# Experts' weights loaded 2 MB at a time into three slots, and other weights stored in whole pieces per partition

## Chip, cores and metric

The kernel runs on 1 core of one Trainium2 chip. The metric is the device time of one execution in microseconds. All inputs lie in the chip's memory (HBM) and are read once per execution, some 763 MB of them.

## What is computed

Two transformer blocks for one sequence of 256 tokens of 1024 features, in float32. The first block is attention and a mixture of 32 experts (each token goes to 4 of them). The second block has two layers, each with three branches (attention, a gated MLP over tokens, a convolution) and an MLP of width 4096; its first layer is also run for 256 context tokens, whose keys and values the latent tokens attend to. Cut to the parts that the change touches:

```python
def moe_ffn(h, ...):                       # 32 experts, top 4, blocks of tokens per expert
    logits = h @ w_router + b_router
    top_val, top_idx = lax.top_k(logits, 4)
    gates = softmax(top_val)
    for each block of tokens of one expert e:
        gu = xe @ w_gate_up[e] + b_gate_up[e]          # 1024 x 2048
        g = minimum(gu[:, :1024], 7); u = clip(gu[:, 1024:], -7, 7)
        act = (u + 1) * (g * sigmoid(1.702 * g))
        y = act @ w_down[e] + b_down[e]                # 1024 x 1024
    return sum over a token's experts of y * gate

def second_block(...):
    for l in range(2):
        p = h @ w_in[l]                                # 1024 x 8704
        x = x + g1 * rms_norm(mixer_merge(p, attn, ...))   # w_attn_o, w_gmlp_o, w_conv_o, w_out: 1024 x 1024
        x = x + g2 * rms_norm(square(relu(h2 @ w1)) @ w2)  # 1024 x 4096, 4096 x 1024
        # for l == 0 the same for the context tokens
```

## The kernel before

The kernel is written on a layer with named tiles in pools; a tag has a number of slots, a tile of a tag that has no free slot waits until the last reader of the oldest one is done, and the layer puts in the semaphores. It also puts each engine's instructions in an order at build time: by priority, and by a model of how long each instruction and transfer takes. On the chip each engine then runs its list in that fixed order. SyncE (SP) issues nearly all weight loads, also in a fixed order, so a load that waits for its slot holds up those behind it.

The work has three parts. The front (L473) is the first block's attention. The experts (`moe`, L998) follow, in the order of `SEQ`, in groups of at most 128 rows. 2 experts have room for 128 tokens, 16 for 64 and 14 for 32 (`CAPS`, sorted by the number of tokens they got; `overflow`, L1016, is run only if that does not suffice). Between the steps of the front and the experts, `prio` (L1702) lets the context pass (`ctx_pass`, L1368, self.side is True) emit its own steps, and gives the front and the experts the higher priority; the context's products are what TensorE does when an expert's weights are not there yet. When the context pass is through, self.solo is True and the experts may use its tiles too. The tail (self.tail) is two layers (`layer`, L1220) one behind the other.

The linear layers (`lin_steps`, L336) take their weights in blocks of 1024 x 512, 2 MB: `load_w` (L303) loads the block, `wsplit` (L317) splits its rows into a high and a low part (ScalarE writes `whi`, VectorE `wlo`; with an "s" at the end for the context pass), and TensorE makes three products of 256 columns of each 128 x 128 piece, at one pass each. A block is 96 such matmuls. The tiles of the weights are `raw` (three slots of 8 KB per partition, 1 MB), `raws` (three of 4 KB) and, for the context pass, `rawx` (one of 4 KB). In the front and in the experts' part a block is two `raw`, in the context pass four `raws` or `rawx`, in the tail one `raw` and two `raws`.

An expert's weights are not split; its products are plain float32. `expert_up` (L934) loads w_gate_up in 8 pieces of 128 rows, 1 MB each (`load_gu`, L917), and for each of them (k) issues the matmuls of L950; `expert_down` (L961) loads w_down in 4 pieces of 256 rows, 1 MB each (`load_dn`, L925), and issues those of L975 for each half of a piece. The tokens are the stationary side, so an expert of 32 tokens uses 32 of the 128 columns of the array, and its output columns go to four such groups side by side; one of 64 tokens uses two groups. The profile shows a float32 matmul as two instructions, so a 1 MB piece is 16 instructions for 32 tokens and 8 for 64 or 128.

`big` (L904) picks the slot of each piece in turn: two tiles of the pool mw (`raw3`, `raw4`) and the three of `raw`, five slots of 1 MB; if solo, five tiles of the context pass (`SPARE`) as well. The same `big` is:

```python
j = self.slot % (spare + len(MORE) + 3)
if j < spare:
    return self.t(self.cx, [P, 2048], tag=SPARE[j])
if j < spare + len(MORE):
    return self.t(self.mw, [P, 2048], tag=MORE[j - spare])
return self.t(self.raw, [P, 2048], tag="raw")
```

All weight matrices lie in HBM as the reference has them, row after row. The part of one partition in a transfer is then a row of 512 columns, 2 KB, for the linear layers, 8 KB (2048 columns) for w_gate_up and 4 KB (1024 columns) for w_down. Each such row is one packet of a DMA engine in the profile.

`combine` (L846) takes a group's results y, multiplies each row by its gate, splits it (`yh`, `yl`), and adds it up over tokens by matmuls against `G`, L873 and L874. `pad` (L117) is a tile that only moves the addresses of those behind it.

Of the kernel before, what the change touches and what calls it, by code (L numbers as in the profile page):

```python
# [98 lines left out]
class Builder:  # L99
    def __init__(self, tc, a, out, dbg=None):  # L100
# [4 lines left out]
        self.fbg = 0  # L105
        self.firstw = []
# [189 lines left out]
    def half(self):  # L296
        if self.side:
            self.hslot += 1
            if self.hslot % 4 == 0:
                return self.t(self.cx, [P, 1024], tag="rawx")  # L300
        return self.t(self.raw, [P, 1024], tag="raws")

    def load_w(self, w, q=None, parts=None):  # L303

        q = q or self.nc.sync
        parts = parts or (2, 1, 1) if self.tail else (1, 1, 1, 1) if self.side else (2, 2)
        rows, k0 = [], 0
        for h in parts:
            n = 2 * h
            r = self.t(self.raw, [P, 1024 * h], tag="raw") if h == 2 else self.half()  # L310
            r = r.rearrange("p (k n) -> p k n", k=n)
            q.dma_start(r, w[k0 * P:(k0 + n) * P, :].rearrange("(k p) n -> p k n", p=P))
            rows += [r[:, i:i + self.wn, :] for i in range(0, n, self.wn)]
            k0 += n
# [76 lines left out]
    def ada_pieces(self, w, b, sT, badd, mod, nv, slots=(), spool=None):  # L391
# [4 lines left out]
        def rows(k):  # L396
# [9 lines left out]
            for g0 in range(0, 4, ng):  # L406
                c0 = b * 2048 + g0 * 512
                r = self.half() if tag == "raws" else self.t(pool, [P, ng * 512], tag=tag, bufs=2 if tag == "gate" else None)
# [64 lines left out]
    def front(self, pool):  # L473
# [29 lines left out]
        w = a["w_in"][0]  # L503

        def project(sec, gi, dst):
            o = self.lin(w[:, sec * 512:(sec + 1) * 512], (hi, lo))
# [23 lines left out]
        def values(sec, v):  # L530
            o = self.lin(w[:, sec * 512:(sec + 1) * 512], (hi, lo), form="A")
# [129 lines left out]
        for s in range(2):  # L661
            o = self.lin(a["w_out"][0][:, s * 512:(s + 1) * 512], (ohi, olo))
# [241 lines left out]
    def big(self, solo):  # L904

        self.slot += 1
        if solo == "only":
            return self.t(self.cx, [P, 2048], tag=SPARE[self.slot % len(SPARE)])
# [107 lines left out]
    def overflow(self, pool):  # L1016
# [3 lines left out]
        with tc.If(anyv > 0):  # L1020
# [9 lines left out]
            with tc.For_i(0, NE, 1) as i:  # L1030
                cv = nc.values_load(self.ovi[0:1, bass.ds(i, 1)], min_val=0, max_val=T)
                with tc.If(cv > 0):
# [4 lines left out]
                    for t in range(2):  # L1037
                        brow = self.t(self.mw, [P, 2048], tag="raw3")
                        nc.sync.dma_start(brow[0:1, :], a["b_gate_up"][0][bass.ds(reg, 1), :])
                        h2 = self.t(self.mw, [P, 2048], tag="raw4")[:, :D].rearrange("p (k t) -> p k t", k=KC)  # L1040
# [179 lines left out]
    def layer(self, l, L, xT, pool, kall, vall, xs, pre=()):  # L1220
# [3 lines left out]
        w = a["w_in_2"][l]  # L1224
# [12 lines left out]
        for s in range(2):  # L1237
            ob = self.lin(w[:, 4608 + s * 512:5120 + s * 512], h, raws=early())
# [5 lines left out]
            oa = self.lin(w[:, 3584 + s * 512:4096 + s * 512], h, raws=early())  # L1244
# [5 lines left out]
        o = self.lin(w[:, 1024:1536], h, form="KV")  # L1250
# [7 lines left out]
        for s in range(2):  # L1258
            o = self.lin(w[:, 2560 + s * 512:3072 + s * 512], h, form="A")
            self.gv_evac(o, gv, gst, s)  # L1260
            o = self.lin(w[:, s * 512:(s + 1) * 512], h)
# [4 lines left out]
        for s in range(2):  # L1266
            o = self.lin(w[:, 1536 + s * 512:2048 + s * 512], h)
# [15 lines left out]
        def branch(goff, wo, acts, first, bg=0):  # L1283
            gts = [self.t(pool, [P, 4, T], tag="gate", bufs=2) for _ in range(2)]
            for s in range(2):
                o = self.lin(w[:, goff + s * 512:goff + (s + 1) * 512], h, bg=bg)
# [530 lines left out]
```

## Time and profile before

| | us |
|---|---|
| median of three runs | 2849.21 |
| lowest and highest | 2847.45, 2853.07 |
| the profiled execution's own time | 2844.92 |
| its span, from the first to the last instruction | 2842.8 |
| mean granted clock of TensorE, as a share of 2.4 GHz | 0.974 |

The profile is of one execution. PE is TensorE's matmuls, PEld its weight loads, DVE VectorE, ACT ScalarE, POOL GpSimd, SP SyncE. Busy time counts from an instruction's start to its end; the ends of matmuls are modelled, and neighbours overlap, so that the distance of two starts tells how fast they follow each other, not the duration. A wait is put down to the event that came last. A DMA share is the mean busy time of the 16 DMA engines over the stretch. L347 is the matmul of the linear layers, L950 and L975 are the experts', L324 and L325 the splits, L312, L921 and L929 the loads of `load_w`, `load_gu` and `load_dn`.

### The profile page before, as it was taken

The page shows a single profiled execution, that of the slowest core. Times are in us where ns is not written, and L with a number is a line of the kernel's source. Part 1 is how long each engine was busy: PE and PEld are TensorE (multiplying, and loading weights), DVE is VectorE, ACT ScalarE, POOL GpSimd, SP SyncE. Part 2 cuts the span into 40 slices and gives each one's busy share as a digit, 9 for nine tenths or more (in the row PEclk, how much of TensorE's full clock was granted, in tenths as well). Part 3 has the DMA queues.
Part 4 walks back from the last instruction along what each step waited for, and adds up shares of the span by engine and source line. Part 5 has one row for each costly group of instructions (what it writes and reads, how often), then busy time and mean ns, then how long its engine had stood idle before and what let it go on. Part 6 is the DMA issues. An engine that isn't in the chain of part 4 may idle for free. (4 is left out here: it accounts for less than half of the span.)

```text
span 2842.8 us, 50509 instructions
## 1 busy us (share of the span) xinstructions
PE 2695.5 (95%) x20396; PEld 2046.5 (72%) x20397; DVE 1635.6 (58%) x3105; ACT 1167.1 (41%) x1988; POOL 310.8 (11%) x300
## 2 busy tenths in 40 slices
PE   7999999999899999999999979899999998999898
PEld 5657777677566777664533338789888997899898
DVE  3564543868534424332321148999655789997655
ACT  2343343433233323221211126675544566666544
POOL 0000000000000000000000005545000045451000
PEclk9989999999799899999999989999999999999999
DMA  9767899899789998988899974435766544345352
GB/s 395 295 240 273 338 367 354 318 362 372 308 333 359 358 354 326 352 307 333 336 378 417 416 290 165 133 112 202 243 210 230 180 154 141 119 148 182 131 198 100
DMA packets 230015, 769.85 MB, mean 271 GB/s; under 512 B 14880, under 2 KB 15264, under 8 KB 189200
## 3 DMA queue, kind: packets, MB, share of 16 engines
q1 hardware_dynamic: 228384, 759.16, 71.9%
q0 software_dynamic: 1392, 7.41, 0.7%
q8 instruction: 162, 2.65, 0.4%
q14 instruction: 77, 0.63, 0.1%
HBM read 762.84 MB, written 3.67 MB: 270 GB/s over the span
## 5 line engine op out<-in xcount | busy, mean ns | idle before, releaser
L347 PE MATMUL lin<-hhi,wlo 128*128 128x256 f32 x1440 | 398.6, 282 | 22.8 <-DVE wlo L325 22.8
L347 PE MATMUL lin<-hhi,whi 128*128 128x256 f32 x1440 | 400.9, 282 | 3.3 <-ACT hhi L283 3.3
L347 PE MATMUL lin<-hlo,whi 128*128 128x256 f32 x1440 | 400.9, 280 | 0.1
L950 PE MATMUL mlin<-raw,hG 128*32 128x256 f32 (+2 forms) x2696 | 365.1, 474 | 3.5 <-DMA raw<-in_w_gate_up_dram 3.5
L325 DVE TENSOR_TENSOR wlo<-raw,whi 128x1024 fp32r<-128x1024 f32 (+1 forms) x232 | 268.0, 1157 | 133.7 <-ACT whi L324 124.5
L325 DVE TENSOR_TENSOR wlos<-raws,whis 128x512 fp32r<-128x512 f32 x246 | 167.9, 689 | 236.9 <-ACT whis L324 205.4
L324 ACT ACTIVATE whi<-raw 128x1024 fp32r<-128x1024 f32 (+1 forms) x232 | 217.8, 941 | 203.1 <-PE lin L347 126.5
L347 PEld LDWEIGHTS lin<-hhi,wlo 128*128 128x128 f32 x1440 | 269.8, 190 | 36.7 <-DVE wlo L325 32.5
L1532 POOL TENSOR_TENSOR yc<-yc,ctmp 128x256 f32<-128x256 f32 x240 | 256.1, 1091 | 296.4 <-ACT ctmp L1531 295.8
L324 ACT ACTIVATE whis<-raws 128x512 fp32r<-128x512 f32 x246 | 153.0, 630 | 313.4 <-PE side L347 297.5
L347 PEld LDWEIGHTS lin<-hhi,whi 128*128 128x128 f32 x1440 | 271.8, 190 | 7.9 <-ACT hhi L283 4.2
L347 PEld LDWEIGHTS lin<-hlo,whi 128*128 128x128 f32 x1440 | 272.9, 190 | 3.0 <-issue 1.4
L325 DVE TENSOR_TENSOR wlo<-raws,whi 128x1024 fp32r<-128x1024 f32 x164 | 206.5, 1259 | 106.5 <-ACT whi L324 106.1
L324 ACT ACTIVATE whi<-raws 128x1024 fp32r<-128x1024 f32 x164 | 174.1, 1062 | 186.4 <-PE lin L347 180.1
L950 PEld LDWEIGHTS mlin<-raw,hG 128*32 128x32 f32 (+2 forms) x2696 | 119.4, 123 | 141.0 <-issue 91.4
L347 PE MATMUL side<-hhi,whis 128*128 128x256 f32 x720 | 204.9, 289 | 0.5 <-ACT hhi L283 0.2
L347 PE MATMUL side<-hlo,whis 128*128 128x256 f32 x720 | 203.1, 286 | 0.0
L347 PE MATMUL side<-hhi,wlos 128*128 128x256 f32 x720 | 199.7, 290 | 1.1 <-DVE wlos L325 1.0
L975 PE MATMUL main<-raw,aT 128*32 128x256 f32 (+2 forms) x1368 | 185.8, 460 | 0.9 <-DMA raw<-in_w_down_dram 0.9
L1534 DVE SCALAR_TENSOR_TENSOR yc<-gl,cw,yc 128x256 f32<-128x256 f32 x240 | 170.9, 748 | 0.1
L347 PEld LDWEIGHTS side<-hhi,whis 128*128 128x128 f32 x720 | 136.9, 190 | 28.4 <-issue 22.6
L347 PEld LDWEIGHTS side<-hhi,wlos 128*128 128x128 f32 x720 | 132.8, 190 | 26.3 <-issue 18.8
(595 smaller groups left out, 5798.2 us busy)
## 6 DMA issues: line engine op xcount, KB each, us to landing
raw<-in_w_gate_up_dram SPq DMA_DIRECT2D x233, 1024.0 KB, 7.4
raw<-in_w_down_dram SPq DMA_DIRECT2D x115, 1024.0 KB, 8.2
raws<-in_w_in_dram SPq DMA_DIRECT2D x119, 512.0 KB, 3.7
raws<-in_w_ff_dram SPq DMA_DIRECT2D x112, 512.0 KB, 4.8
raw<-in_w_in_dram SPq DMA_DIRECT2D x48, 1024.0 KB, 5.2
raw<-in_w_ff_dram SPq DMA_DIRECT2D x32, 1024.0 KB, 5.5
phi<-in_ada_w_dram SPq DMA_DIRECT2D x10, 1024.0 KB, 7.5
plo<-in_ada_w_dram SPq DMA_DIRECT2D x10, 1024.0 KB, 7.1
```

Of the source, the lines that this page charges most:

```text
L324: x = nc.scalar.activation(flat(hi), flat(rows[i]), AF.Copy)
L325: y = nc.vector.tensor_sub(flat(lo), flat(rows[i]), flat(hi).bitcast(F32))
L347: x = nc.tensor.matmul(*args, skip_group_check=True, **kw)
L950: nc.tensor.matmul(d, hT(k), gu[k][c0 // D][:, c0 % D:c0 % D + W], start=False, stop=(k == KC - 1), skip_group_check=True)
L975: nc.tensor.matmul(pys[h][g * C:(g + 1) * C, :W], st, dn[m][:, c0:c0 + W], start=(m == 0), stop=(m == KC - 1), skip_group_check=True)
L1532: nc.gpsimd.tensor_add(d, d, m)
L1534: self.paced(1, nc.vector.scalar_tensor_tensor(d, x, wcol, d, op0=OP.mult, op1=OP.add))
```

## The change

It has four parts, here in the order of the code.

1. `load_gu` and `load_dn` load two k of w_gate_up, or four 128-row blocks of w_down, in one DMA of 2 MB. `big` gives three slots of 16 KB per partition: `raw3` in mw (in place of `raw3` and `raw4`) and two `raw`. The five tiles of the context pass, used when solo, stay at 8 KB and take one k or two blocks each.
2. Every weight matrix of the linear layers is stored in HBM as blocks of 1024 x 512 with each partition's 8 pieces one behind the other (`blocks`), and w_down with the four 128-row pieces of a half together. A partition's part of a transfer is then 4 KB for a `raws` piece, 8 KB for a 1 MB half of a block, 16 KB for w_down.
3. `load_w` takes a block as one 16 KB tile of `raw` in two DMAs of 1 MB; in the context pass as four small pieces as before; in the tail every third block as four small pieces and the others whole. `raw8` cuts a `raw` tile in two for the adaptive-norm weights.
4. The expert pool gets a pad of 64 bytes behind its first y tile, and the scratch of the software DMA queue is 4096 bytes instead of 8192.

```diff
@@ Builder
-    def load_w(self, w, q=None, parts=None):
+    def raw8(self):
+        if self.second is None:
+            x = self.t(self.raw, [P, 2, 2048], tag="raw")
+            self.second = x[:, 1, :]
+            return x[:, 0, :]
+        x, self.second = self.second, None
+        return x
+
+    def wblk(self, name, l, col, row=0):
+        return self.a[name][l, row // D, col // 512]
+
+    def load_w(self, w, q=None):
         q = q or self.nc.sync
-        parts = parts or (2, 1, 1) if self.tail else (1, 1, 1, 1) if self.side else (2, 2)
+        small = self.side
+        if self.tail:
+            self.nblock += 1
+            small = self.nblock % 3 == 0
+        whole = None if small else self.t(self.raw, [P, 4096], tag="raw")
         rows, k0 = [], 0
-        for h in parts:
+        for h in (1, 1, 1, 1) if small else (2, 2):
             n = 2 * h
-            r = self.t(self.raw, [P, 1024 * h], tag="raw") if h == 2 else self.half()
+            r = self.half() if small else whole[:, k0 * 512:(k0 + n) * 512]
             r = r.rearrange("p (k n) -> p k n", k=n)
-            q.dma_start(r, w[k0 * P:(k0 + n) * P, :].rearrange("(k p) n -> p k n", p=P))
+            q.dma_start(r, w[:, k0:k0 + n, :])
@@ setup
-        self.raw = st.enter_context(tc.tile_pool(name="raw", bufs=3))
+        self.raw = st.enter_context(tc.tile_pool(name="raw", bufs=2))
...
-            o = self.lin(w[:, sec * 512:(sec + 1) * 512], (hi, lo))
+            o = self.lin(self.wblk("w_in", 0, sec * 512), (hi, lo))
@@ big
-        j = self.slot % (spare + len(MORE) + 3)
+        j = self.slot % (spare + 3)
         if j < spare:
-            return self.t(self.cx, [P, 2048], tag=SPARE[j])
-        if j < spare + len(MORE):
-            return self.t(self.mw, [P, 2048], tag=MORE[j - spare])
-        return self.t(self.raw, [P, 2048], tag="raw")
+            return self.t(self.cx, [P, 1, 2048], tag=SPARE[j])
+        if j == spare:
+            return self.t(self.mw, [P, 2, 2048], tag="raw3")
+        return self.t(self.raw, [P, 2, 2048], tag="raw")
 
     def load_gu(self, eng, e, solo):
         gu = []
-        for k in range(KC):
+        while len(gu) < KC:
+            k = len(gu)
             r = self.big(solo)
-            eng.dma_start(r, self.a["w_gate_up"][0][bass.ds(e, 1), k * P:(k + 1) * P, :].rearrange("o p f -> p (o f)"))
-            gu.append([r[:, :D], r[:, D:]])
+            n = min(r.shape[1], KC - k)
+            eng.dma_start(r[:, 0:n, :], self.a["w_gate_up"][0][bass.ds(e, 1), k * P:(k + n) * P, :].rearrange(
+                "o (k p) f -> p (o k) f", p=P))
+            gu += [[r[:, i, :D], r[:, i, D:]] for i in range(n)]
         return gu
 
     def load_dn(self, eng, e, solo):
         dn = []
-        for j in range(4):
-            r = self.big(solo)
-            eng.dma_start(r.rearrange("p (k n) -> p k n", k=2), self.a["w_down"][0][
-                bass.ds(e, 1), j * T:(j + 1) * T, :].rearrange("o (k p) n -> p (o k) n", p=P))
-            dn += [r[:, :D], r[:, D:]]
+        while len(dn) < KC:
+            k = len(dn)
+            r = self.big(solo).rearrange("p a (k n) -> p (a k) n", n=D)
+            n = min(r.shape[1], 4 - k % 4)
+            eng.dma_start(r[:, 0:n, :], self.a["w_down"][bass.ds(e, 1), k // 4, :, k % 4:k % 4 + n, :].rearrange(
+                "o p k n -> p (o k) n"))
+            dn += [r[:, i, :] for i in range(n)]
         return dn
@@ moe
             y = self.t(pool, [P, D], tag="y")
+            if g == 0:
+                self.pad(pool, 64)
@@ host
+def blocks(z):
+    n, r, c = z.shape
+    return z.reshape(n, r // D, KC, P, c // 512, 512).transpose(0, 1, 4, 3, 2, 5)
...
+    for n in _BLOCKS:
+        host[n] = blocks(host[n])
+    host["w_down"] = host["w_down"].reshape(NE, 2, 4, P, D).transpose(0, 1, 3, 2, 4)
...
-    nc = bacc.Bacc("TRN2", target_bir_lowering=False, num_devices=1, dynamic_dma_scratch_size=8192)
+    nc = bacc.Bacc("TRN2", target_bir_lowering=False, num_devices=1, dynamic_dma_scratch_size=4096)
```

## Rows read from the trace of the kernel before

**Rows 1.** The page, part 1: busy us (share of the span) xinstructions

```profile
PE 2695.5 (95%) x20396; PEld 2046.5 (72%) x20397; DVE 1635.6 (58%) x3105; ACT 1167.1 (41%) x1988; POOL 310.8 (11%) x300
```

**Rows 2.** Stretches: length, busy time of each engine (instructions), PEclk, DMA share, GB/s

```profile
0.00:300.00 300.00, 271.38 (x1847) 190.16 (x1849) 154.79 (x537) 103.82 (x220) 6.75 (x22) 0.93 0.78 295
300.00:1450.00 1150.00, 1127.74 (x8819) 756.63 (x8820) 540.36 (x1166) 362.93 (x677) 1.31 (x4) 0.98 0.91 345
1450.00:1670.00 220.00, 200.63 (x962) 74.68 (x958) 40.74 (x78) 26.43 (x44) 0.00 (x0) 0.99 1.01 412
1690.00:2843.00 1153.00, 1086.94 (x8738) 1019.77 (x8738) 888.92 (x1308) 666.86 (x1037) 300.94 (x269) 0.98 0.49 165
```

**Rows 3.** Waits of TensorE, 300 to 1450: us in total, times, longest us

```profile
PE side L1576 <- DVE y L1534: 9.0, 1, 9.0
```

**Rows 4.** Waits of SyncE's queue, 300 to 1450

```profile
SPq L921 <- PE main L975: 178.1, 83, 7.1
SPq L921 <- PE mlin L950: 156.8, 72, 10.7
```

**Rows 5.** Timeline of TensorE: start, us, instruction, xcount, [idle before <-releaser]

```profile
1461.83 1.94 PE L950 MATMUL mlin<-raw,hG 128*64 128x512 f32 x8 [0.56 <-DMA raw<-in_w_gate_up_dram]
1464.32 1.94 PE L950 MATMUL mlin<-raw,hG 128*64 128x512 f32 x8 [0.54 <-DMA raw<-in_w_gate_up_dram]
```

**Rows 6.** Waits of TensorE and of SyncE's queue, 1690 to 2843

```profile
PE lin L347 <- DVE wlo L325: 28.6, 34, 1.8
...
SPq L312 <- DVE wlo L325: 770.9, 188, 22.5
```

**Rows 7.** Timeline of TensorE around one single run and one double run

```profile
319.16 0.28 PE L347 MATMUL side<-hhi,wlos 128*128 128x256 f32 x1
319.28 0.28 PE L347 MATMUL side<-hhi,whis 128*128 128x256 f32 x1
319.49 1.07 PE L950 MATMUL mlin<-raw,hG 128*32 128x256 f32 x16
320.49 0.39 PE L347 MATMUL side<-hlo,whis 128*128 128x256 f32 x1
320.71 0.28 PE L347 MATMUL side<-hhi,wlos 128*128 128x256 f32 x1
...
1004.73 0.28 PE L347 MATMUL side<-phi,wlos 128*128 128x256 f32 x1
1004.93 1.93 PE L950 MATMUL mlin<-raw,hG 128*32 128x256 f32 x32
1006.80 0.39 PE L347 MATMUL side<-phi,whis 128*128 128x256 f32 x1
1007.02 0.28 PE L347 MATMUL side<-plo,whis 128*128 128x256 f32 x1
```

**Rows 8.** Timeline of TensorE: first and last of the counted runs

```profile
465.99 1.94 PE L950 MATMUL mlin<-raw,hG 128*64 128x512 f32 x8
...
1183.65 1.07 PE L975 MATMUL main<-raw,aT 128*32 128x256 f32 x16
...
1442.49 1.94 PE L975 MATMUL main<-raw,aT 128*64 128x512 f32 x8
```

**Rows 9.** DMA issues, 300 to 1450: engine, op xcount, KB each, median us to landing

```profile
raw<-in_w_gate_up_dram SPq DMA_DIRECT2D x201, 1024.0 KB, 7.2
raw<-in_w_down_dram SPq DMA_DIRECT2D x96, 1024.0 KB, 7.6
```

**Rows 10.** Waits of ScalarE, 0 to 300

```profile
ACT whi L324 <- DMA raw<-in_w_in_dram: 6.5, 2, 5.5
```

**Rows 11.** DMA of the whole execution: a queue (packets, MB, share), issues (as rows 9)

```profile
q0 software_dynamic: 1392, 7.41, 0.7%
...
raws<-in_w_in_dram SPq DMA_DIRECT2D x119, 512.0 KB, 3.7
```

**Rows 12.** One line's instructions: durations in ns, min/median/max, first and last start

```profile
L873 PE MATMUL main<-G,yh x80: 277/282/388, 522.1 to 1456.9; 128*128 128x256 f32 x72, 64*128 64x256 f32 x8
```

More of the change, by code (lines that the diff above doesn't have):

```diff
@@ L105, in __init__ @@
         self.fbg = 0
+        self.nblock, self.second = 0, None
         self.firstw = []
@@ L407, in rows @@
                 c0 = b * 2048 + g0 * 512
-                r = self.half() if tag == "raws" else self.t(pool, [P, ng * 512], tag=tag, bufs=2 if tag == "gate" else None)
+                if tag == "raws":
+                    r = self.half()
+                elif tag == "raw":
+                    r = self.raw8()
+                else:
+                    r = self.t(pool, [P, ng * 512], tag=tag, bufs=2 if tag == "gate" else None)
                 x = nc.sync.dma_start(r, w[k * P:(k + 1) * P, c0:c0 + ng * 512])
@@ L530, in values @@
         def values(sec, v):
-            o = self.lin(w[:, sec * 512:(sec + 1) * 512], (hi, lo), form="A")
+            o = self.lin(self.wblk("w_in", 0, sec * 512), (hi, lo), form="A")
             for t in range(2):
@@ L661, in front @@
         for s in range(2):
-            o = self.lin(a["w_out"][0][:, s * 512:(s + 1) * 512], (ohi, olo))
+            o = self.lin(self.wblk("w_out", 0, s * 512), (ohi, olo))
             for j in range(2):
@@ L1223, in layer @@
         nc, a = self.nc, self.a
-        w = a["w_in_2"][l]
+        w = lambda c: self.wblk("w_in_2", l, c)
         v = 0
@@ L1243, in layer @@
                 self.kv()
-            oa = self.lin(w[:, 3584 + s * 512:4096 + s * 512], h, raws=early())
+            oa = self.lin(w(3584 + s * 512), h, raws=early())
             for j in range(2):
@@ L1306, in layer @@
         for s in range(2):
-            o = self.lin(a["w_out_2"][l][:, s * 512:(s + 1) * 512], (mhi, mlo))
+            o = self.lin(self.wblk("w_out_2", l, s * 512), (mhi, mlo))
             for j in range(2):
@@ L1362, in layer @@
             o = []
-            steps = self.lin_steps(o, a["w_in_2"][1][:, 1024:1536], self.hc, form="KV")
+            steps = self.lin_steps(o, self.wblk("w_in_2", 1, 1024), self.hc, form="KV")
             self.fill.extend([lambda: next(steps)] * 4)
@@ L1370, in ctx_pass @@
         nc, a = self.nc, self.a
-        w = a["w_in_2"][0]
+        w = lambda c: self.wblk("w_in_2", 0, c)
         v = 1
@@ L1397, in ctx_pass @@
         kc, vc = kvc[:, 0:2, :], kvc[:, 2:4, :]
-        o = self.lin(w[:, 1024:1536], h, form="KV")
+        o = self.lin(w(1024), h, form="KV")
         self.k_evac(o[0], L, kc, False, cx)
@@ L1413, in branch @@
                 yield
-                o = self.lin(wo[:, s * 512:(s + 1) * 512], acts)
+                o = self.lin(self.wblk(wo, 0, s * 512), acts)
                 self.merge(merged, gt, o, s, first)
@@ L1469, in ctx_pass @@
         for s in range(2):
-            o = self.lin(w[:, 2560 + s * 512:3072 + s * 512], h, form="A")
+            o = self.lin(w(2560 + s * 512), h, form="A")
             self.gv_evac(o, gv, gst, s)
@@ L1478, in ctx_pass @@
         yield from conv(1)
-        yield from branch(6656, a["w_gmlp_o_2"][0], (phi, plo), False)
+        yield from branch(6656, "w_gmlp_o_2", (phi, plo), False)
         phi, plo = pair()
@@ L1482, in ctx_pass @@
         yield
-        yield from branch(7680, a["w_conv_o_2"][0], (phi, plo), False)
+        yield from branch(7680, "w_conv_o_2", (phi, plo), False)
         phi, plo = pair()
@@ L1488, in ctx_pass @@
         for s in range(2):
-            o = self.lin(a["w_out_2"][0][:, s * 512:(s + 1) * 512], (phi, plo))
+            o = self.lin(self.wblk("w_out_2", 0, s * 512), (phi, plo))
             for j in range(2):
@@ L1507, in ctx_pass @@
                 c0 = f * D + s * 512
[L1508 removed]
+                o = self.lin(self.wblk("w_ff1_2", 0, c0), (hi, lo))
                 self.relu2(o, phi, plo, s, cx)
@@ L1750, in build @@
                         self.tail, self.wn = True, 2
-                        w = a["w_in_2"][0]
-                        pre = [self.load_w(w[:, 4608:5120]), self.load_w(w[:, 3584:4096], parts=(2, 2))]
+                        w = lambda c: self.wblk("w_in_2", 0, c)
+                        pre = [self.load_w(w(4608)), self.load_w(w(3584))]
                         self.tail = False
```

51 lines of the change are left out of this document (25 added, 26 removed).

## The prediction, put on record before the changed kernel was run

> **What bounds the kernel now.** I read the page's busy line first [rows 1]: matmuls cover 95% of the span, which by itself says little, since their ends are modelled. So I split the span into stages [rows 2]. From 0 to 300 us (front layer) the transfers run at a share of 0.78. From 300 to 1450 us the experts are worked through, with the context layer's products as filler ("side" tiles): matmuls are busy 1127.7 of 1150 us, transfers 0.91. From 1450 to 1670 us only experts are left: transfers are at 1.01 and 412 GB/s, matmuls have gaps. From 1690 us on the two tail layers run with transfers at 0.49.
>
> Then I asked, for each stage, which wait ends last. In 300 to 1450 TensorE's longest wait is one of 9.0 us behind VectorE [rows 3], and in that whole answer no row tells of a wait that a transfer ended. The other direction is full: SyncE's queue stands 178.1 + 156.8 = 335 us in front of w_gate_up loads until a matmul lets a slot go [rows 4]. So the weights are there early, and the stage lasts as long as TensorE's own stream of instructions. In 1450 to 1670 it is the reverse: every step of 1 MB begins after a wait for its load, and steps come 2.49 us apart though one lasts 1.94 us [rows 5]. In the tail it is TensorE, and VectorE's weight splits, 28.6 us in 34 waits; SyncE there waits 770.9 us for those splits [rows 6]. So only the middle stage and the experts-only stage can gain from the way in which experts are loaded.
>
> **Part 1: two steps of an expert per load (load_gu, load_dn, big).** What the middle stage's stream is made of shows in the timeline [rows 7]. Experts with 32 or 64 tokens use the array in 32- or 64-column tiles, the side products use all 128 columns. One load's worth of tiled work (16 instructions) stands between two runs of full-width ones. From the last side matmul before it (319.28) to the second after it (320.71) are 1.43 us: two side slots and 16 instructions. Where two loads' worth happen to stand together (x32), the same distance is 1004.73 to 1007.02 = 2.29 us. Side matmuls follow each other every 0.12 us (319.16, 319.28). Two single runs with their four side slots are 2.86 us; one double run, two side slots of its own and two more are 2.29 + 0.24 = 2.53 us. So each pair that is joined saves 0.33 us: that is what going into a tiled run and out of it costs.
>
> How many are there: in the timeline of 300 to 1450 us I count 125 runs of exactly x16 at 128*32 and 69 of exactly x8 at 128*64, both one load's worth; the first are at 319.49 [rows 7] and 465.99, the last at 1183.65 and 1442.49 [rows 8]. The unit is the load, not the step of the loop: for w_gate_up it is one k, for w_down two, and both give the same run length. The order on TensorE is written at build time by a planner that lets high-priority expert work in when its data should be there, so I expect the unit to follow the load: now two k, or four. 194 singles become 97 pairs: 97 x 0.33 = 32 us off a stage in which nothing else is late. Bounds: 0 (side matmuls still go in between the two halves) and, if longer runs form, half of all 273 tiled loads of the stage (297 loads [rows 9] less 24 of the two 128-token experts): 137 x 0.33 = 45 us. I take 32, because the rows show the load as the unit in both kinds.
>
> What comes due next: transfers would have to deliver the same bytes in 1118 us instead of 1150, a share of 0.94 for 0.91, less what longer rows save. That fits below the 1.01 of the experts-only stage.
>
> A 2 MB slot has to land whole before its first half is used, 1 MB more at 412 GB/s = 2.5 us later than now. Cover: three slots of 2 MB instead of five of 1 MB, so that between 4 and 6 MB stand ahead of TensorE instead of 4 to 5, and the queue's 335 us of standing still [rows 4]. I cost it at nothing; what it costs without cover is the slower rival.
>
> **Part 2: rows in whole pieces (blocks, wblk, the w_down layout).** Transfer time per byte follows from shares [rows 2]: the tail, nearly all 2 KB rows, moves 165/0.49 = 337 GB/s at full share; the experts-only stage, 8 KB and 4 KB rows, 412/1.01 = 408. After the change side weights come in 4 KB rows, tail and front weights in 8 KB, w_down in 16 KB. It pays only where transfers bind. In the 220 us from 1450 on, the 4 KB third becomes 16 KB: between 0 and 21% (the whole distance 337 to 408) of a third, 0 to 15 us; nearer to 0, as the step from 4 to 16 KB is the upper end of that distance. I take 5 us, less some 2 us, because one 1 MB step (1.94 us, [rows 5]) more remains behind the last landing: 3. In the front layer ScalarE waits 6.5 us for w_in in all [rows 10]: I take 2 us of 0 to 6.5, about the share that 8 KB rows save of a 2 KB row's time. In the middle and the tail nothing, since the queue waits for slots there.
>
> **Part 3: slots of the tail (load_w).** Two blocks of three come as one 16 KB tile, every third as four pieces in three slots, so its last piece can be issued only when its own first piece has been split, and the following blocks' loads stand behind it on SyncE. A block is four quarters of 24 matmuls at 0.12 us, so the piece is due 3 x 2.9 = 8.6 us after the first; such pieces land in 3.7 us [rows 11], with a 2 MB load at 412 GB/s in front in 8.8. I take 0, since the splits run up to three buffers ahead of TensorE; bounds -5 and, without that cover, some 27 such blocks (a third of the 83 of the two layers) x 1 us = +27 us.
>
> **Part 4: the small ones.** The 64-byte pad in the expert pool moves the combined results against their gates. The combine matmuls last 282 ns in the median and 277 at the least [rows 12]; with some 220 of them that is 1 us at most, either way: nothing. The smaller scratch of the software queue: its transfers are 0.7% of the engines' time [rows 11], 20 us spread over the span, and few are waited for: nothing, bound +5 us for one 1 MB transfer in line.
>
> **Sum.** 32 + 3 + 2 + 0 = 37 us. The profiled execution took 2844.9 us (span 2842.8 and 2.1 around it), 4.3 below the median of the three runs; against the median, 2849.2 - 37 = 2812 us.
>
> **Rivals.** (a) The forecast, 0.55: 2812, with its own bounds (20 to 45 for the joins, the rest as taken) 2799 to 2824.
> (b) Transfers, not TensorE, bind the middle stage, 0.12. For it: weight loads are busy only 756.6 of 1150 us there, against 1019.8 of 1153 in the tail [rows 2], so the array is not full. Against it: no wait on a transfer [rows 3]. Then joins give nothing, and the cheaper rows do: 345 GB/s x 1150 us less 297 loads of 1.05 MB leaves 85 MB of other weights, in 2 KB rows; going half the way from 337 to 408 GB/s they save 85 x (2.97 - 2.69) = 24 us; with 5 from the other stages 2820.
> The Trainium skill's page "Perfetto Trace Analysis", section "Identifying the Most-Contended Engine", speaks for this one: matmul busy time is not a good measure of TensorE, the busy share of its weight loads is, and by that 66% is not a bound. The waits are why I leave it at 0.12.
> (c) The runs do not join: the planner puts side matmuls between the halves as before, 0.18. Then 3 + 2 are left: 2844, half of it within 0.2%.
> (d) Slower, 0.15: the coarser slot starves TensorE. A slot is given back after two steps instead of one, SyncE stands in front of it twice as long, and the side weights queue up behind it. There are 297/2 = 149 such loads in the middle stage; from 0.25 us of TensorE idle per load (37/149) the gain is gone, at 0.5 us the time is 2812 + 74 = 2886. Against it: the 335 us of queue time, which is slack now.
>
> **How the numbers follow.** Faster or slower counts from 0.2% (5.7 us), about what a measurement of this kernel can tell from no change. Faster: 0.55 + 0.12 + 0.09 of (c) = 0.76. Same: 0.09. Slower: 0.15. The range takes in (a) to (c) with their bounds, from 2849 - 45 - 15 = 2789 up to no gain at all with 2 us of part 4, 2851; it leaves out (d).
>
> **What would show it.** Right: in the middle stage the tiled runs are x32 and x16 and about half as many; the start of the experts-only stage comes some 32 us earlier; distances within a run stay; the tail's length stays within 5 us. Wrong: single-step runs as many as now (c); a run count that halves while the stage keeps its length (b); rows of TensorE or of the side splits waiting for a transfer in that stage (d); or a tail that is longer by more than 10 us (part 3).

## The result and the profile after

The changed kernel takes 2814.15 us (median of 4 runs, 2808.83 to 2832.73), the one before 2849.53 us (median of 4). The ratio is 0.9894, with a 95% interval of 0.9869 to 0.9918: 30 us less, between 23 and 37 (the medians alone are 35 us apart). The prediction was 2812 us. The profiled execution took 2815.26 us, 29.7 us less than the profiled one of before.

In the changed kernel L365 is the matmul of the linear layers, L976 and L1001 are the experts', L342 and L343 the splits, L330, L944 and L955 the loads of `load_w`, `load_gu` and `load_dn`. First the stretches of the changed kernel, which answer to [rows 2] (columns as there):

```profile
0.00:300.00 300.00, 273.36 (x1821) 188.89 (x1823) 152.82 (x521) 104.79 (x221) 6.88 (x23) 0.93 0.75 290
300.00:1450.00 1150.00, 1117.00 (x8959) 765.14 (x8958) 549.52 (x1196) 366.96 (x682) 1.31 (x4) 0.98 0.91 357
1450.00:1670.00 220.00, 190.40 (x917) 78.24 (x916) 51.99 (x106) 33.94 (x57) 1.79 (x5) 0.94 0.91 375
1690.00:2843.00 1153.00, 1060.71 (x8538) 993.06 (x8536) 875.57 (x1274) 652.87 (x1020) 301.91 (x269) 0.99 0.44 161
```

Between 300 and 1450 us there are 140 more matmuls than before in the same time, at the same transfer share of 0.91 (357 GB/s for 345). Why shows in the timeline of TensorE (start, us, instruction, count), around the first loads of an expert; it answers to [rows 7]:

```profile
324.24 0.28 PE L365 MATMUL side<-hhi,wlos 128*128 128x256 f32 x1
324.35 0.28 PE L365 MATMUL side<-hhi,whis 128*128 128x256 f32 x1
324.56 1.93 PE L976 MATMUL mlin<-raw,hG 128*32 128x256 f32 x32
326.43 0.39 PE L365 MATMUL side<-hlo,whis 128*128 128x256 f32 x1
326.65 0.28 PE L365 MATMUL side<-hhi,wlos 128*128 128x256 f32 x1
```

Two steps stand together, and from the last side matmul before them to the second after them are 2.30 us, as for the rare double run of before (2.29). Counted from the timeline up to the last side product of a linear layer, there are 171 column-tiled runs of the experts' matmuls (with the bias products ahead of them); before there were 259. The single runs (x16 at 128*32, x8 at 128*64) are gone, but for one.

The waits in 300 to 1450 us, of TensorE on a transfer and of SyncE's queue on a slot (us in total, times, longest; the queue's answer to [rows 4]):

```profile
PE mlin L976 <- DMA raw<-in_w_gate_up_dram: 1.7, 3, 0.9
...
SPq L944 <- PE main L1001: 181.5, 42, 17.1
SPq L944 <- PE mlin L976: 144.1, 43, 9.1
```

By these two rows the queue still stands 326 us in front of w_gate_up loads (335 before), and TensorE waits 1.7 us for one.

When things begin and end, from the timeline of TensorE (starts, except where the row says end; us):

| | before | after | |
|---|---|---|---|
| first matmul of an expert | 309.5 | 324.6 | +15.0 |
| last side product of a linear layer | 1424.8 | 1415.4 | -9.4 |
| end of the last matmul of an expert | 1673.9 | 1644.4 | -29.5 |
| first matmul of the tail | 1693.5 | 1664.1 | -29.4 |
| end of the last matmul | 2834.0 | 2804.8 | -29.2 |

So the whole gain lies ahead of the tail: 24.4 us between the first expert's matmul and the last side product, 20.1 us in the experts-only stage behind it (249 to 229 us), and 15.0 us given back ahead of it.

### The profile page after: what moved, and what is told of

Its sections match the earlier page's. It is cut to its first block, busy times and chain, and to the rows that moved or that the text cites. A ratio compares the mean times of both kernels' runs of the same rounds, so it can differ in the third digit from the quotient of the medians.

```text
span 2813.5 us, 49773 instructions
## 1 busy us (share of the span) xinstructions
PE 2661.5 (95%) x20396; PEld 2045.3 (73%) x20397; DVE 1639.8 (58%) x3105; ACT 1167.3 (41%) x1988; POOL 311.9 (11%) x301
## 5 line engine op out<-in xcount | busy, mean ns | idle before, releaser
L343 DVE TENSOR_TENSOR wlo<-raw,whi 128x1024 fp32r<-128x1024 f32 (+1 forms) x288 | 337.4, 1174 | 160.4 <-ACT whi L342 153.2
L365 PE MATMUL lin<-hhi,wlo 128*128 128x256 f32 x1440 | 398.3, 283 | 20.8 <-DVE wlo L343 20.5
L365 PE MATMUL lin<-hhi,whi 128*128 128x256 f32 x1440 | 399.6, 281 | 2.2 <-ACT hhi L284 2.2
L365 PE MATMUL lin<-hlo,whi 128*128 128x256 f32 x1440 | 400.7, 280 | 0.1
L342 ACT ACTIVATE whi<-raw 128x1024 fp32r<-128x1024 f32 (+1 forms) x288 | 277.2, 964 | 257.9 <-PE lin L365 185.2
L976 PE MATMUL mlin<-raw,hG 128*32 128x256 f32 (+2 forms) x2720 | 348.3, 463 | 6.4 <-DMA raw<-in_w_gate_up_dram 6.3
L343 DVE TENSOR_TENSOR wlos<-raws,whis 128x512 fp32r<-128x512 f32 x246 | 167.7, 689 | 223.3 <-ACT whis L342 203.2
L365 PEld LDWEIGHTS lin<-hhi,wlo 128*128 128x128 f32 x1440 | 269.5, 190 | 36.2 <-DVE wlo L343 32.2
L365 PEld LDWEIGHTS lin<-hhi,whi 128*128 128x128 f32 x1440 | 271.5, 190 | 5.6 <-ACT hhi L284 3.7
L365 PEld LDWEIGHTS lin<-hlo,whi 128*128 128x128 f32 x1440 | 272.8, 189 | 2.8 <-issue 1.4
L342 ACT ACTIVATE whis<-raws 128x512 fp32r<-128x512 f32 x246 | 152.1, 629 | 280.1 <-PE side L365 246.2
L976 PEld LDWEIGHTS mlin<-raw,hG 128*32 128x32 f32 (+2 forms) x2720 | 126.8, 122 | 165.2 <-issue 117.4
L365 PE MATMUL side<-hhi,whis 128*128 128x256 f32 x720 | 203.4, 288 | 1.6 <-ACT hhi L284 1.1
L365 PE MATMUL side<-hlo,whis 128*128 128x256 f32 x720 | 200.3, 283 | 0.0
L365 PE MATMUL side<-hhi,wlos 128*128 128x256 f32 x720 | 193.7, 286 | 1.1 <-DVE wlos L343 1.0
L343 DVE TENSOR_TENSOR wlo<-raws,whi 128x1024 fp32r<-128x1024 f32 x108 | 138.4, 1281 | 71.6 <-ACT whi L342 70.8
L1001 PE MATMUL main<-raw,aT 128*32 128x256 f32 (+2 forms) x1336 | 174.0, 458 | 0.2 <-SPq L1048 0.2
L342 ACT ACTIVATE whi<-raws 128x1024 fp32r<-128x1024 f32 x108 | 114.5, 1060 | 122.4 <-PE lin L365 103.0
L365 PEld LDWEIGHTS side<-hhi,whis 128*128 128x128 f32 x720 | 136.3, 189 | 16.0 <-issue 11.3
L365 PE MATMUL side<-phi,whis 128*128 128x256 f32 x512 | 143.9, 287 | 2.2 <-ACT whis L342 1.8
```

Source lines behind the costliest of these rows:

```text
L342: x = nc.scalar.activation(flat(hi), flat(rows[i]), AF.Copy)
L343: y = nc.vector.tensor_sub(flat(lo), flat(rows[i]), flat(hi).bitcast(F32))
L365: x = nc.tensor.matmul(*args, skip_group_check=True, **kw)
L976: nc.tensor.matmul(d, hT(k), gu[k][c0 // D][:, c0 % D:c0 % D + W], start=False, stop=(k == KC - 1), skip_group_check=True)
L1001: nc.tensor.matmul(pys[h][g * C:(g + 1) * C, :W], st, dn[m][:, c0:c0 + W], start=(m == 0), stop=(m == KC - 1), skip_group_check=True)
```

## Experiments

The runs fall into three questions: is it the joined runs, what do they need, and what did the other parts do. In this table "runs" are the tiled runs up to the last side product, "gate_up by 1200" is the number of w_gate_up instructions on TensorE between 300 and 1200 us, "last side" and "last expert" are as in the table above, and the tail's length is from its first matmul to the end of the last one; all are counted from each kernel's timeline.

| kernel | ratio to before (95%) | runs | gate_up by 1200 | last side | last expert | tail's length |
|---|---|---|---|---|---|---|
| before | 1 | 259 | 2134 | 1424.8 | 1673.9 | 1140.5 |
| the change | 0.9894 (0.9869 to 0.9918) | 171 | 2176 | 1415.4 | 1644.4 | 1140.7 |
| e1: pairs, five slots of 1 MB | 0.9980 (0.9966 to 0.9994) | 143 | 2112 | 1258.4 | 1665.7 | 1145.0 |
| e2: single loads, three slots of 2 MB | 1.0013 (0.9996 to 1.0030) | 254 | 2176 | 1446.9 | 1677.5 | 1139.2 |
| e13: e2, y8 last | 0.9960 (0.9943 to 0.9977) | 254 | 2176 | 1448.2 | 1664.6 | 1141.4 |
| e5: single loads, six slots of 1 MB | 1.0049 (1.0020 to 1.0077) | 268 | 2176 | 1475.7 | 1684.5 | 1145.0 |
| e6: pairs, six slots of 1 MB | 0.9975 (0.9956 to 0.9995) | 178 | 2176 | 1420.9 | 1658.5 | 1142.7 |
| e12: e6, y8 last | 0.9896 (0.9874 to 0.9918) | 178 | 2176 | 1424.1 | 1645.4 | 1144.6 |
| e4: quads, three slots of 2 MB | 1.0450 (1.0420 to 1.0479) | 84 | 1984 | 1196.5 | 1803.3 | 1142.1 |

### e1: joined runs alone

`k` in the kernel before runs 1, 0, 3, 2, ...; `m` of w_down 2, 3, 0, 1, ...:

```diff
-        for k in range(KC):
+        for n in range(KC):
+            k = n ^ 1
...
-        for m in range(KC):
+        for n in range(KC):
+            m = n ^ 2
```

> The kernel before, with its 1 MB loads, its five slots and its old rows; only the order of the steps of an expert is changed: step 1 before step 0, 3 before 2, and so on (of w_down the second load's two steps before the first's). So the first matmul of a pair waits for the later of two loads, and the other step is ready behind it. In the order of TensorE's instructions there are then 144 column-tiled runs up to the last side product, against 260 before and 169 after. Theory J (what is saved is the way into and out of a tiled run, 0.33 us each): 116 x 0.33 = 38 us less than before, 2811 us, as fast as the change or faster, with none of its 2 MB loads and none of its layout. Rival L (the larger load or the slot is what helps): no change, 2849 us. Rival S (waiting for the second load of a pair starves TensorE): slower than before, by 0.25 us for each of about 150 pairs, 2886 us.

Measured: 2841.72 us, ratio 0.9980. The runs are joined (143 of them, fewer than in the change), and 6 us come of it, not 38: nearer to rival L (no change) than to theory J. Rival S (slower) falls. The stretches of e1, cut at its own last side product (columns as in [rows 2]):

```profile
309.00:1258.00 949.00, 926.77 (x8005) 685.06 (x7998) 496.65 (x1051) 345.12 (x645) 0.77 (x3) 0.98 0.91 350
1258.00:1666.00 408.00, 360.93 (x1704) 142.18 (x1703) 78.91 (x168) 43.96 (x74) 0.54 (x1) 0.97 0.94 378
```

TensorE is through with the side products 166 us earlier than before, but the experts' steps come no earlier: by 1200 us 2112 instructions of w_gate_up are done, against 2134, and the 3000th matmul of the experts starts at 1170.5 us, against 1160.0. The rows of that line alone, in 300 to 1200 us, of before, e1 and the change (length, PE, PEld, PEclk, DMA share, GB/s):

```profile
300.00:1200.00 900.00, 229.57 (x2134) 83.98 (x2135) 0.97 0.92 350
...
300.00:1200.00 900.00, 205.55 (x2112) 85.12 (x2112) 0.98 0.92 354
...
300.00:1200.00 900.00, 229.95 (x2176) 96.08 (x2176) 0.98 0.92 361
```

So the saved time was filled with side products ahead of their turn. When these had run out, 1184 of the experts' 4416 matmul instructions were left, against 784 before and 704 in the change, and the experts were then alone for 407 us instead of 249, with matmuls busy for 361 of 408 us. The saving was real and was given back in the next stage. Theory J as it stood (fewer switches, shorter kernel) falls: it needs a condition.

### e2 and e13: the change without joined runs

Each 16 KB slot is filled by two loads of 1 MB, so that a step can start with its own half (`load_dn` likewise):

```diff
-            eng.dma_start(r[:, 0:n, :], ...[bass.ds(e, 1), k * P:(k + n) * P, :]...)
+            for i in range(n):
+                eng.dma_start(r[:, i:i + 1, :], ...[bass.ds(e, 1), (k + i) * P:(k + i + 1) * P, :]...)
```

> The changed kernel with its three 16 KB slots and its layout, but each slot is filled by two loads of 1 MB, so that a step can start when its own half is there. The order of TensorE then has 253 tiled runs up to the last side product, against 169 of the changed kernel. Theory J: 84 x 0.33 = 28 us more than the changed kernel, 2842 us. Rival L (fewer slots of double size, or the layout, bring the gain and the runs do not matter): 2814 us, or faster, since the first half is there earlier.

Measured: 2851.25 us, 37 us over the change, with 254 runs: more than the 28 us of theory J; rival L (2814 us) falls. Here the experts are as early as in the change (2176 by 1200 us), but the last side product comes 31.5 us later. Part of the 37 us was something else: SyncE's queue stood 34.1 us in front of a load into y8, a tile that the context pass was still using, and TensorE then waited 11.1 us (waits from 1400 to 1500 us; `y` is y8, the view leaves numbers out):

```profile
SPq L945 <- DVE hks L1706: 34.1, 1, 34.1
...
PE mlin L978 <- DMA y<-in_w_gate_up_dram: 11.1, 1, 11.1
```

e13 takes that away by another order of the five context tiles (`SPARE`), with y8 first in the list, so that it is reached later:

```diff
-SPARE = ("phi", "plo", "hhi", "hlo", "y8")
+SPARE = ("y8", "phi", "plo", "hhi", "hlo")
```

> The changed kernel with two loads of 1 MB per 16 KB slot (2851 us), and the context pass's tiles in the order y8, phi, plo, hhi, hlo, so that the queue's 34.1 us in front of y8 and TensorE's 11.1 us behind it are gone. 253 tiled runs in the order. Theory J (the runs themselves cost 0.33 us each): 2851 - 11 = 2840 us, still 26 us over the changed kernel's 2814. Rival K2 (all that the single loads lost was that stop): 2814 us.

Measured: 2837.85 us, ratio 0.9960; expected 2840, and rival K2 (2814 us) falls. TensorE's long wait is gone; the queue still stands 11.7 us at that tile. Against the change that is 24 us for 83 more runs. The closer comparison is e14 below (2811.37 us), the change with the same order of the five tiles: it differs from e13 in the loads alone, and it is 26.5 us faster, 0.32 us per run. So with these slots the joins carry most of the change's gain; but joins were worth 6 us in e1. What differs is the slots.

### e5, e6 and e12: one MB more of slots

The kernel before with a fourth `raw` tile, six slots of 1 MB, first with single steps, then with the pairs of e1:

```diff
-        self.raw = st.enter_context(tc.tile_pool(name="raw", bufs=3))
+        self.raw = st.enter_context(tc.tile_pool(name="raw", bufs=4))
...
-        j = self.slot % (spare + len(MORE) + 3)
+        j = self.slot % (spare + len(MORE) + 4)
```

> The kernel before with a sixth slot of 1 MB for the experts (a fourth raw tile of 8 KB, paid for with the smaller scratch of the changed kernel); single loads of 1 MB, old rows, the tail's pattern as before (with four raw slots instead of three). 273 tiled runs in the order, against 260. Theory B (two bounds: the slots pace the experts, and TensorE's sum of work sets how late the side products end; one alone gives nothing): the 3000th matmul of the experts comes some 40 us earlier than before's 1160 us, as in the run with single loads (1118.6), but the last one ends within 6 us of before's 1674 us, as there (1677); the total is 2847 us, less what the fourth slot gives in the tail (0 to 11 us). Rival A (the slots alone are the gain): the experts end at about 1644 us, total 2817 us or less.

> The sixth slot and the paired order of steps together, still with loads of 1 MB, old rows and the old tail pattern; 183 tiled runs in the order. Theory B: both bounds move, and the experts end where they end in the changed kernel, at about 1644 us, 30 us earlier than before: 2817 us, or down to 2806 if the fourth slot helps the tail. Rival G (it takes loads of 2 MB, pairs of 1 MB loads don't do): as with pairs and five slots, 2842 us.

Measured: 2864.33 us for e5 and 2840.21 for e6, both above what theory B expected, and e6 where rival G has it. Yet the experts' pace did what it said: 2176 by 1200 us in both, as in every kernel with 6 MB of slots and steps in ones or twos, and the 3000th matmul of the experts at 1115 us. What came between shows in the waits of e6 from 1420 to 1500 us, of TensorE and of the queue:

```profile
PE mlin L951 <- DMA raw<-in_w_gate_up_dram: 17.2, 2, 16.0
...
SPq L921 <- DVE hks L1677: 29.2, 1, 29.2
```

The queue stands in front of the load into y8 until VectorE's last step of the context pass (hks); in e5 it stands 18.9 us there, and TensorE then waits 11.0 us. Behind it stand all other loads, though their slots are free: five `raw` loads go out right behind it (timeline of SyncE in e6: start, us, load, count):

```profile
1431.65 0.34 SPq L921 DMA_DIRECT2D hlo<-in_w_gate_up_dram  x1
1461.39 0.33 SPq L921 DMA_DIRECT2D y<-in_w_gate_up_dram  x1
1461.97 2.92 SPq L921 DMA_DIRECT2D raw<-in_w_gate_up_dram  x5
```

The transfers of e6 from 1435 to 1465 us, 40 slices of 0.75 us (busy tenths):

```profile
DMA  9999999999920000000000000000000000007399
```

They stand still for some 18 us (24 slices). In the kernel before and in e1 the queue comes to that tile when the context pass is long through; in e2, e5, e6 and e11, and for 5.2 us in the change, it does not. e12 is e6 with y8 moved:

```diff
-SPARE = ("phi", "plo", "hhi", "hlo", "y8")
+SPARE = ("y8", "phi", "hhi", "hlo", "plo")
```

> Six slots of 1 MB and pairs as in the run with both (2840 us), but the five tiles of the context pass come in another order (y8, phi, hhi, hlo, plo), so that the load into y8 is not the third of them: SyncE's queue stood 29.2 us in front of it there, until the context pass's last step was done, and TensorE then waited 16.0 us for w_gate_up. 183 tiled runs, as there. Theory K (joins and a sixth MB of slots are all that is needed; that stop is what took the gain back): no wait of more than 4 us on w_gate_up after 1420 us, the experts end at about 1643 us, 2840 - 16 = 2824 us. Rival G (loads of 2 MB are needed): 2840 us.

Measured: 2819.35 us, ratio 0.9896, 21 us less than e6 and the change's own 0.9894 again: loads of 1 MB, rows as before, the tail's pieces as before, no pad. TensorE's long wait is gone, though the queue still stands 12.0 us for hks, and the experts end at 1645.4 us, in the change at 1644.4. (The profiled execution of e6 was its fastest, 2831 us, so the traces show 13 of the 21 us.) Theory K holds and rival G falls: the change's gain takes neither 2 MB loads nor another layout, but joined steps, a sixth MB, and an order in which y8 does not stop the queue for long. Like for like it is not settled whether 2 MB loads and the layout add something: e14, with y8 first too, is 8 us faster than e12, and the two intervals overlap.

Side by side, against before: joins alone (e1) 6 us, 6 MB alone (e13, which has the new layout, too) 11 us, both (e12) 30 us. Together they give more than the sum of each alone.

### e4: longer runs

Pairs of 2 MB loads in the changed kernel:

```diff
-        for k in range(KC):
+        for n in range(KC):
+            k = n ^ 2
...
-        for m in range(KC):
+        for n in range(KC):
+            m = n ^ 4
```

> The changed kernel with the order of its steps swapped in pairs of loads: steps 2, 3, 0, 1, 6, 7, 4, 5 of w_gate_up, steps 4 to 7 before 0 to 3 of w_down. The first matmul waits for the second of two 2 MB loads, and four steps (eight of w_down) follow in one run. The order has 82 tiled runs up to the last side product against 169. Theory J: 87 x 0.33 = 29 us less than the changed kernel, 2785 us, faster than both. Rival S (coarser use of the three slots starves TensorE): two of the three slots are held until four steps are through, so only 2 MB stand ahead; with 75 such quads in the middle stage, 0.4 us of idle TensorE for each takes the gain back (2814), and 1 us makes it 2860.

Measured: 2977.36 us, 163 us over the change: rival S, and far beyond its 2860. There are 84 runs, half the change's, and only 1984 instructions of w_gate_up by 1200 us. The side products end at 1196.5 us, and the experts are then alone for 607 us. Of the experts' instructions 1536 are left at that point (704 in the change). TensorE's waits there, 1200 to 1800 us, and the stretch 1200 to 1700 us of e4 and then of the change (columns as in [rows 2]):

```profile
PE mlin L977 <- DMA raw<-in_w_gate_up_dram: 52.7, 16, 8.3
PE main L1003 <- DMA raw<-in_w_down_dram: 31.5, 8, 5.0
...
1200.00:1700.00 500.00, 388.18 (x1703) 160.59 (x1701) 74.48 (x166) 43.52 (x77) 0.54 (x1) 0.85 0.72 286
...
1200.00:1700.00 500.00, 467.15 (x2560) 244.13 (x2560) 155.65 (x291) 104.31 (x169) 9.93 (x14) 0.97 0.88 349
```

By the edit a quad holds two of the three slots until its four steps are through, and transfers are at 0.72 (0.88 in the change). The granted clock falls to 0.85 as well, so not all of the 163 us are waits. It is e1 once more, with less ahead.

### e3 and e15: the layout

e3 stores all weights as before in the changed kernel (the diff); e15 gives the kernel before the new layout (`blocks`, `wblk` and the w_down layout) and nothing else.

```diff
-            q.dma_start(r, w[:, k0:k0 + n, :])
+            q.dma_start(r, w[k0 * P:(k0 + n) * P, :].rearrange("(k p) n -> p k n", p=P))
```

> The changed kernel with all weights stored as before (rows of 2 KB for the linear layers' pieces, 4 KB for w_down); loads, slots and the order's 169 tiled runs stay. Theory J, with the prediction's part 2: 5 us in the experts-only stage and 2 in the front, 2814 + 7 = 2821 us; the middle stage and the tail keep their lengths within 3 us. Rival T (transfers bind the middle stage, too): 24 + 5 us, 2843 us. A tail that is longer by x us would say that the layout paid for x us of part 3 there.

> The kernel before with the changed layout of the weights alone: five slots, single loads of 1 MB, the tail's pieces and the scratch as before, no pad. 260 tiled runs in the order, as before. By the prediction's part 2: 5 us in the experts-only stage and 2 in the front, 2847 - 7 = 2840 us. Rival R (the change with old rows was 13 us slower, and that is the rows' price): 2834 us. Rival N (those 13 us were the slower pace of TensorE, 117.8 instead of 113.3 ns per matmul, at the end of that run; rows are worth nothing): 2847 us.

Measured: e3 2826.87 us (0.9921, interval 0.9896 to 0.9946), e15 2846.80 us (0.9991, interval 0.9976 to 1.0005). e15 says 2.6 us, between 7 and none, so rival R (13 us) falls; rival T of e3 (2843 us) falls, too. The 13 us of e3 lie, in its profiled execution, in the tail alone: its experts end at 1644.4 us as in the change, its tail is 1151.8 us long, and up to the 5760th matmul of the tail it is as fast (886.5 against 886.2 us). From there on each matmul is slower, as the section on the hardware shows. The intervals of e3 and of the change overlap, so the layout's worth is not settled closer than by e15.

The tail's stretch 1690 to 2800 us of before and of e15 (columns as in [rows 2]) shows that the rows' length did nothing there:

```profile
1690.00:2800.00 1110.00, 1055.51 (x8467) 988.96 (x8468) 867.78 (x1276) 652.04 (x1017) 298.90 (x267) 0.99 0.50 169
...
1690.00:2800.00 1110.00, 1058.58 (x8474) 991.58 (x8475) 867.73 (x1268) 652.08 (x1017) 300.06 (x267) 0.98 0.51 169
```

With 2 KB rows the transfers are at 0.50 and 169 GB/s, with 4 and 8 KB rows at 0.51 and 169. Share and rate in this stretch do not come from the rows' length.

### e8, e11 and e14: the tail's pieces, and the rest

e8 gives the changed kernel's tail its old pieces of 1, 0.5 and 0.5 MB:

```diff
-        if self.tail:
-            self.nblock += 1
-            small = self.nblock % 3 == 0
...
-        for h in (1, 1, 1, 1) if small else (2, 2):
+        for h in parts or ((2, 1, 1) if self.tail else (1, 1, 1, 1) if self.side else (2, 2)):
```

> The changed kernel, but the tail's blocks come in the pieces of the kernel before (1 MB, 0.5, 0.5), the 1 MB piece as half of a 16 KB tile. The experts and the layout are those of the change. Theory P3 (the change's slots in the tail cost some 11 us, which its layout gives back: with the old rows its tail is 11 us longer than before's): the tail, from the first tail matmul to the last, falls from 1140.7 to about 1129 us, total 2803 us. Rival (the tail is bound by TensorE and the splits, whatever the slots): 2814 us.

Measured: 2810.75 us (0.9874, interval 0.9845 to 0.9903); its tail is 1141.3 us long, the change's 1140.7. Theory P3 was built on e3's long tail, and falls with it: the tail does not depend on the pieces.

e11 is e6 with the new layout (and the change's tail rows in the old pieces).

> Six slots of 1 MB with single loads, paired order of steps, the changed layout, the tail's pieces of before: the change without its 2 MB loads and without its tail pattern. 183 tiled runs in the order. Theories B and P3 together: experts' end at about 1644 us, tail of about 1129 us, 2803 us, faster than both kernels by 11 us or more. Rival G (2 MB loads are needed): 2830 us (the pairs with five slots, 2842, less 11).

Measured: 2840.93 us (0.9973). That is above both theories. It is e6 again, with the same stop (29.3 us of the queue, 16.1 us of TensorE), and the layout did not make up for it. What it was meant to tell, e12 tells.

e14 is the change with the `SPARE` of e13.

> The changed kernel with the context pass's tiles in the order y8, phi, plo, hhi, hlo; all else as it is, 169 tiled runs in the order. In the changed kernel the queue stands 6.2 us in front of the load into y8, and the transfers idle there. Theory W (in the experts-only stage transfers bind, so what the queue waits is lost): 2814 - 6 = 2808 us. Rival (the next wait, 13.0 us for a gather's matmuls, ends last anyway): 2814 us.

Measured: 2811.37 us (0.9863, interval 0.9841 to 0.9884), the lowest ratio of all kernels here. Against the change's 0.9894 it is 3 us of median or 9 of ratio, and the intervals overlap: the run does not decide between theory W and its rival. The change's stop at y8 was short (5.2 us of the queue), and in e14 it is gone. The smaller scratch and the pad were not tried alone: the larger slots need the scratch's room.

## Why the prediction was right, and where it was not

**What bounds the kernel.** "The stage lasts as long as TensorE's own stream of instructions" [rows 3, 4] was half of it. That no transfer is waited for shows that TensorE hardly ever waits, not that less work on it ends the stage earlier: it can be filled with work that belongs later. e1 takes more runs away than the change does and gains 6 us. The Trainium skill's page "Perfetto Trace Analysis", section "Identifying the Most-Contended Engine", says that matmul busy time is no good measure of TensorE and the busy share of its weight loads is; by that the stage, with 756.6 us of them in 1150 [rows 2], had room. e1 agrees: its stage has 685 us of them in 949, 72% for 66%. Rival (b), for which the rule spoke, fell as it was priced (e15).

**Part 1, the price.** 0.33 us per join is right: 2.30 us for a double run in the change against two singles of 1.43 [rows 7], and 0.32 us of total time per run between e13 and e14, which differ in nothing else but the size of the loads. The Trainium skill's page "TensorEngine Tiling (Array Packing)", section "Key Properties", says that a change of tiling mode drains TensorE; it has no duration. These rows show what going in and out costs, but not whether a drain is the cause.

**Part 1, the count.** Predicted 97 joins, found 88 (259 to 171): 29 us for 32. The load as the planner's unit was right; e2 has 254 runs with the same slots and half the load.

**Part 1, the cover.** This is the step that failed, though the sum did not show it. "Three slots of 2 MB instead of five of 1 MB" was costed at nothing, as a risk without a price. It was the condition of the gain. By the prediction's own price e1 should have taken 2811 us, and it took 2842. With 5 MB of slots the written order lets 2112 to 2134 w_gate_up instructions in by 1200 us, with 6 MB 2176 (the 3000th matmul of the experts comes at 1160 us in the kernel before and at 1115 in the change), and only with these is there expert work to put into the time that joins set free. "What comes due next" asked whether transfers could follow (share 0.94; it is 0.91), and not whether the filler would run out.

**"The start of the experts-only stage comes some 32 us earlier".** Wrong: 9.4 us. By the prediction's own signs, a run count that falls while the stage nearly keeps its length pointed to (b). The experts start 15.0 us later (86 more matmuls of side products and a later routing ahead of them; which part of the change does that is open, e12 and e5 have 5.8 and 5.5 us of it), and the stage itself is 20.1 us shorter, because more of the experts' work is done by then (704 instructions left, 784 before). The prediction gave that stage 3 us.

**Part 2.** Predicted 5 us, measured 2.6 (none to 7). The size can stand, the reason cannot: the price of 2 KB rows was read from the tail's 337 GB/s at full share [rows 2], and e15 shows that share and rate stay with longer rows.

**Parts 3 and 4.** Predicted 0 for the tail, measured +0.2 us (1140.5 to 1140.7). The bound of +27 us was never near: old pieces or new, the tail keeps its length (e8, 1141.3). The combine matmuls' median is 280 ns against 282 [rows 12], nothing, as said.

**The rivals.** (c), no joins, would have been the result of e2. (b) fell as priced: e15 gained 2.6 us, not 24 and 5. That transfers do not hold TensorE's stream back in the middle stage shows in e1, which was through with the same side products 166 us earlier; the experts' own steps came no faster there. (d) did not come in the change (1.7 us of TensorE waiting for a load), but its mechanism is real: e4 shows its place and is 163 us slower. It decides when a run needs two of three slots.

So the total was right by some luck: the change brought the sixth MB along with the joins, and the prediction put nearly all of the gain down to the joins.

## What to carry to other kernels

Where one engine alternates two streams, time saved on it shortens the kernel only if the stream that ends last can use it: look at which stream runs out first, and give the loads of the other one more slot together with the saving. Joined runs need no larger transfers; swapping neighbouring steps of a sum, so that the later load is waited for first, does the same for a few lines. In a queue that issues loads in order, sort the slots by when they come free: one load into a tile still in use stopped all transfers for 18 us.

## What was not expected of the hardware

TensorE has two paces at the same granted clock. The timeline of the tail of the change, and then of e3; the two rows of each fence are 16 matmuls apart:

```profile
2729.74 0.28 PE L365 MATMUL lin<-shi,whi 128*128 128x256 f32 x1
...
2731.55 0.28 PE L365 MATMUL lin<-shi,wlo 128*128 128x256 f32 x1
```

```profile
2729.82 0.28 PE L365 MATMUL lin<-slo,whi 128*128 128x256 f32 x1
...
2731.70 0.28 PE L365 MATMUL lin<-shi,wlo 128*128 128x256 f32 x1
```

That is 1.81 us in the change and 1.88 in e3, 113 and 118 ns a matmul. The stretch 2700 to 2800 us of e3 and of the change (columns as in [rows 2]) has a granted clock of 1.00 in both, the 2.4 GHz level, and 851 against 880 matmuls:

```profile
2700.00:2800.00 100.00, 100.00 (x851) 100.00 (x850) 59.49 (x61) 46.63 (x52) 0.00 (x0) 1.00 0.44 153
...
2700.00:2800.00 100.00, 99.72 (x880) 99.52 (x879) 59.74 (x63) 47.74 (x57) 2.04 (x2) 1.00 0.39 145
```

In e3 the slower pace holds from about 2550 us to the end, and its tail is 11 us longer; in e5 it holds for the last 200 us. It does not come with the old rows in the tail: e14, which has the new ones, has it for the first 100 us of the tail, and the kernel before, with old rows, has both paces. This is the slower one there, at 2600 us (16 matmuls apart, 1.88 us):

```profile
2599.88 0.28 PE L347 MATMUL lin<-slo,whi 128*128 128x256 f32 x1
...
2601.76 0.28 PE L347 MATMUL lin<-shi,wlo 128*128 128x256 f32 x1
```

What sets it is open. What it adds is as large as many of the differences asked for here, so the length of a stage in a single profile is known no closer than to some 11 us.
